# Last stage of a two-layer inference step: kept weight pieces, layer norm on VectorE, sample rows with the second projection

## Chip, cores and metric

The kernel runs on one core of one Trainium2 chip. The metric is the device time of one execution in microseconds, as the median of the runs.

## What is computed

One inference step of a two-layer model for a prompt of 1024 tokens and a group of 8 sample tokens, with the same weights. Only the second layer's end matters here: the recurrent mixer (RWKV-7) gives an output `y` for each token, gated by `silu(z)`, then comes one output projection by `w_out` (1024 x 1024), a residual and a layer norm.

```
def step(S, inp):                       # recurrence over the tokens, 16 heads of 64 x 64
    r_t, w_t, k_t, v_t, kk_t, a_t = inp
    sa = einsum('bhvk,bhk->bhv', S, kk_t)
    S = S * w_t[:, :, None, :] - sa[..., None] * (kk_t * a_t)[:, :, None, :] + v_t[..., None] * k_t[:, :, None, :]
    return S, einsum('bhvk,bhk->bhv', S, r_t)
...
out = (y.reshape(B, T, D_C) * silu(z)) @ w_out
...
xp = _layer_norm(ALPHA * xp + yp, ln_g[l], ln_b[l])    # prompt, 1024 rows
xq = _layer_norm(ALPHA * xq + ys, ln_g[l], ln_b[l])    # samples, 8 rows

def _layer_norm(x, g, b, eps=1e-5):
    mu = x.mean(-1); var = square(x - mu).mean(-1)
    return (x - mu) * rsqrt(var + eps) * g + b
```

## The kernel before

The kernel has four phases; the change lies in the last, `phase_d`, the second layer. It has two streams of work.

**The recurrence** runs in 16 units: 128 tokens (`g` = 0 to 7) by half of the heads (`d` = 0, 1). Each unit goes through generators: `s1` and `s2` prepare its matrices (`AM`, `BK`, `MRB`, `SV`, `KBK` and others, tiles of the unit pool `us` with three buffers, or of `up` with one), `joinUT` inverts a triangle, and `s3` carries the state `ST` through the unit in two chunks of 64 tokens. A chunk ends with the VectorE multiplication at L1547 (into `SV` after the first chunk, into `ST` after the second); a unit ends with its normed output `sq` (L1562, L1563), which goes to DRAM as `YT`, or, for the last unit, stays as `G.Y`.

**The projections** are generators in a list `F1`, from which the loop over the units takes about one step for each step of a unit: the gate projection for 512 tokens (`t_proj(.., "z", ..)`, into `SZ`) and `t_out(0)`, then again one and `t_out(1)`; `t_out(2)` joins the list at unit 13, `t_last` at unit 15. `t_out(g)` projects 256 tokens. It loads the recurrence's output (`og`) and the gate (`xs`) in 8 blocks of 128 features, multiplies and splits them in a high and a low part (`xh`, `xl`), and then goes over two halves `f` of the output and four pieces `k2` of the weights. For each piece, `wsplit` (L1172) loads 512 KB of `w_out` into a tile `w`, ScalarE makes the high part `wh` (L113) and GpSimd, or each third time VectorE, the low part `wl` (L121); three products of 512 columns follow for each row tile and k step (L1772 to L1774): `xh wh`, `xh wl`, `xl wh`. The pool of the weights has two buffers of each name. VectorE joins the sum with the residual (L1777) into the tile `big` and sums the rows; `ln_out` does the layer norm, with gain and bias rows loaded into tiles `w` of the same pool. In `t_out(2)` the 8 sample rows come along as a third row tile: 264 columns in place of 256, products into `sm`, residual and result in `xk`.

`t_last` does the last 256 tokens. They end only with the last unit, so it works on two tiles of 128 tokens: for the first tile, `tis` is (0,) throughout; the second goes with it for the pieces with `k2` under 2 and comes last for the other four, for which the four pieces are loaded and split again once `G.Y` is there (L1728). Its gain and bias rows lie in tiles `KBK` and `AM`.

The layer norm of a row tile before: mean; ScalarE's Square with a sum (L1655, its unneeded result in a tile `og`); variance; ScalarE's Ln and Exp (L1659, L1660), each with a table load ahead; three small VectorE operations; then over 1024 columns a VectorE pass for subtraction and scale (L1665), and two passes for gain (L1666) and bias (L1667), on GpSimd but for the last tile of `t_last`. Row tiles come one after the other.

The order of instructions on each engine is not written by hand: a scheduler goes over the generators' instructions with a model of their times and fixes one order for each engine, and each engine takes its queue in order. SP issues almost all loads and stores.

## Time and profile before

| | us |
|---|---|
| three runs | 2203.44, 2210.73, 2210.95 |
| median | 2210.73 |
| profiled execution | 2201.91 |
| its span | 2200.2 |

TensorE is busy for 1844.0 us of the span, VectorE for 1491.9, ScalarE for 1153.6 and GpSimd for 972.8. The mean granted clock of TensorE is 0.871 of full speed. The stage that the change touches begins at about 1826 us, when `t_out(0)` comes to its layer norm. The second projection's last join is at 1993, the third's at 2087, the recurrence's last output comes at 2162, and the program ends at 2200. In the rows further below, `PE` is TensorE, `DVE` VectorE, `ACT` ScalarE, `POOL` GpSimd, and `SPq` the queue of SyncE, which issues DMAs; a name left of an arrow is the tile written, those right of it are read.

### The profile page before, as it was taken

To read this page: it belongs to the slowest core of one execution; us is meant where nothing else is said; L and a number is where in the kernel's file an instruction comes from. 1 tells how busy PE (TensorE), PEld (TensorE's weight loads), DVE (VectorE), ACT (ScalarE), POOL (GpSimd) and SP (SyncE) were. 2 spreads that over 40 slices of the span, in tenths; PEclk is the share of its full clock that TensorE was granted. 3 is DMA by queue.
4 is the path that set the end of the run, shared out by engine and by line. 5 is a ranking of instruction groups with operands and counts; after the bars stand their busy time and mean duration, and the time that the engine had idled before them with its cause. 6 is when DMAs were issued, how large, how long until landed. Compare 5 with 4: busy or idle time off the path is not lost. (4 is left out here: it accounts for less than half of the span.)

```text
span 2200.2 us, 41365 instructions
## 1 busy us (share of the span) xinstructions
PE 1844.0 (84%) x16026; PEld 1545.8 (70%) x16026; DVE 1491.9 (68%) x2543; ACT 1153.6 (52%) x2359; POOL 972.8 (44%) x784
## 2 busy tenths in 40 slices
PE   5988897668999997897887999897999787987865
PEld 5987896656767886674777987695888666875543
DVE  5998995557788878226364378827748987387453
ACT  3323324544665545357466467747754575465344
POOL 4667667554655545445345212323334434113233
PEclk9998998867999876898898999897899986988956
DMA  6424344521221213546556344433544544353333
GB/s 240 132 72 142 131 151 154 200 74 33 65 59 50 58 34 97 175 126 210 167 179 204 126 118 116 145 100 117 149 130 121 180 115 135 97 155 115 119 112 103
DMA packets 232095, 275.27 MB, mean 125 GB/s; under 512 B 71545, under 2 KB 171569, under 8 KB 227738
## 3 DMA queue, kind: packets, MB, share of 16 engines
q1 hardware_dynamic: 210712, 215.21, 32.1%
q0 software_dynamic: 7616, 41.52, 5.6%
q10 hardware_dynamic: 13570, 15.90, 2.0%
q8 instruction: 126, 2.06, 0.4%
q14 instruction: 71, 0.58, 0.1%
HBM read 212.47 MB, written 64.27 MB: 126 GB/s over the span
## 5 line engine op out<-in xcount | busy, mean ns | idle before, releaser
L121 POOL TENSOR_TENSOR wl<-w,wh 128x1024 fp32r<-128x1024 f32 x81 | 200.2, 2473 | 333.5 <-ACT wh L113 317.8
L1184 PE MATMUL mm<-xh,wh 128*128 128x256 f32 (+1 forms) x1024 | 308.3, 302 | 22.6 <-ACT og L1319 9.3
L1185 PE MATMUL mm<-xl,wh 128*128 128x256 f32 (+1 forms) x1024 | 300.9, 294 | 2.0 <-POOL xl L1212 1.1
L1186 PE MATMUL mm<-xh,wl 128*128 128x256 f32 (+1 forms) x1024 | 298.5, 293 | 3.5 <-POOL wl L121 3.5
L113 ACT ACTIVATE wh<-w 128x1024 fp32r<-128x1024 f32 (+2 forms) x130 | 134.4, 1036 | 208.2 <-PE mm L1185 60.9
L1184 PEld LDWEIGHTS mm<-xh,wh 128*128 128x128 f32 x1024 | 201.9, 198 | 35.8 <-ACT og L1319 12.0
L1185 PEld LDWEIGHTS mm<-xl,wh 128*128 128x128 f32 x1024 | 203.2, 198 | 5.4 <-issue 2.0
L1186 PEld LDWEIGHTS mm<-xh,wl 128*128 128x128 f32 x1024 | 202.1, 198 | 6.3 <-POOL wl L121 4.4
L268 DVE SCALAR_TENSOR_TENSOR c<-U,cw,c 128x1024 f32<-128x1024 f32 x120 | 198.0, 1674 | 0.9
L604 POOL TENSOR_TENSOR Pl<-PT,Ph 128x512 fp32r<-128x512 f32 (+1 forms) x102 | 131.9, 1298 | 150.4 <-DVE Ph L603 123.9
L252 POOL TENSOR_TENSOR cbuf<-cbuf 128x256 f32<-128x256 f32 (+2 forms) x72 | 131.3, 1829 | 85.2 <-ACT cbuf L250 82.3
L217 PE MATMUL S<-xh,wh 128*128 128x344 f32 (+1 forms) x432 | 146.6, 339 | 21.1 <-ACT wh L113 19.4
L219 PE MATMUL S<-xh,wl 128*128 128x344 f32 (+1 forms) x432 | 145.4, 337 | 15.7 <-POOL wl L121 11.6
L218 PE MATMUL S<-xl,wh 128*128 128x344 f32 (+1 forms) x432 | 146.3, 339 | 3.8 <-POOL xl L121 3.6
L1212 POOL TENSOR_TENSOR xl<-xs,xh 128x520 fp32r<-128x520 f32 (+1 forms) x76 | 104.6, 1382 | 91.2 <-ACT xh L1211 89.1
L250 ACT ACTIVATE cbuf<-cbuf,wrow 128x256 f32<-128x256 f32 x192 | 79.3, 496 | 112.1 <-DMA cbuf<-in_ccmp,cix 70.3
L1208 DVE SCALAR_TENSOR_TENSOR xs<-xk,mu,xs 128x512 f32<-128x512 f32 x96 | 92.7, 973 | 56.4 <-ACT xs L1207 55.7
L217 PEld LDWEIGHTS S<-xh,wh 128*128 128x128 f32 (+1 forms) x432 | 85.6, 198 | 23.2 <-ACT wh L113 21.9
L562 DVE TENSOR_REDUCE nm<-S 128x1 f32<-128x640 f32 (+7 forms) x128 | 88.3, 699 | 18.9 <-PE S L558 17.7
L219 PEld LDWEIGHTS S<-xh,wl 128*128 128x128 f32 (+1 forms) x432 | 84.9, 197 | 20.1 <-POOL wl L121 13.6
L121 DVE TENSOR_TENSOR wl<-w,wh 128x1024 fp32r<-128x1024 f32 x45 | 60.4, 1341 | 54.1 <-ACT wh L113 53.9
L218 PEld LDWEIGHTS S<-xl,wh 128*128 128x128 f32 (+1 forms) x432 | 84.8, 196 | 7.1 <-POOL xl L121 4.4
(610 smaller groups left out, 5399.3 us busy)
## 6 DMA issues: line engine op xcount, KB each, us to landing
w<-in_w_rkvz SPq DMA_DIRECT2D x64, 512.0 KB
w<-in_w_out SPq DMA_DIRECT2D x36, 512.0 KB
w<-in_w_fm SPq DMA_DIRECT2D x25, 512.0 KB
xk<-x1T SPq DMA_DIRECT2D x48, 260.0 KB
xk<-x1T SPq DMA_DIRECT2D x48, 256.0 KB
w<-in_w_out SPq DMA_DIRECT2D x16, 256.0 KB
x<-in_xp SPq DMA_DIRECT2D x8, 512.0 KB
x<-x ACTq DMA_DIRECT2D x8, 512.0 KB
```

The costliest lines, as they stand in the source:

```text
L113: nc.scalar.activation(hi, src, AF.Copy, **({} if scale is None else {"scale": scale}))
L121: e_lo.tensor_tensor(lo, src, hi, op=SUB)
L217: nc.tensor.matmul(dst, lhsT=wh[:, k, 0:n], rhs=xh[:, k, sl], start=k == 0, stop=False)
L218: nc.tensor.matmul(dst, lhsT=wh[:, k, 0:n], rhs=xl[:, k, sl], start=False, stop=False)
L219: nc.tensor.matmul(dst, lhsT=wl[:, k, 0:n], rhs=xh[:, k, sl], start=False, stop=k == 7)
L252: nc.gpsimd.tensor_tensor(bv[:, 0:n], bv[:, 0:n], bv[:, n:2 * n], op=ADD)
L268: e.scalar_tensor_tensor(c[:, i, 0:T], u[:, k:k + T], cwh[:, i, k:k + 1], c[:, i, 0:T], op0=MUL, op1=ADD)
L604: lambda: nc.gpsimd.tensor_tensor(Pl[:, 0:w], PT[:, 0:w], Ph[:, 0:w], op=SUB)]
L1184: nc.tensor.matmul(dst, lhsT=wh[:, k], rhs=xh[k][:, lo:hi], start=k == 0, stop=False)
L1185: nc.tensor.matmul(dst, lhsT=wh[:, k], rhs=xl[k][:, lo:hi], start=False, stop=False)
L1186: nc.tensor.matmul(dst, lhsT=wl[:, k], rhs=xh[k][:, lo:hi], start=False, stop=k == 7)
L1212: (nc.vector if early[0] and k % LD == 0 else nc.gpsimd).tensor_tensor(lo[k][:, 0:n], t[:, 0:n], hi[k][:, 0:n], op=SUB)
```

## The change

Four things are changed, all in `phase_d`:

1. `wsplit` can write into tiles that are handed to it. `t_last` takes eight tiles of the unit pool (two each of `MRB`, `BK`, `SV` and `AM`) and keeps in them the split parts of the four pieces with `k2` of 2 and 3, so that the second tile uses these again: 8 loads and splits in place of 12. Its gain and bias rows move to tiles `w`.
2. `ln_out` goes over all row tiles stage by stage: all Squares, all Ln, all Exp. Two VectorE passes take the place of the three: (x - mean) times gain, then times the scale plus bias. The first is written ahead of the small operations on the scale, and GpSimd does nothing here any more.
3. The sample rows go with `t_out(1)` in place of `t_out(2)`.
4. At the start of `t_out(1)` the sample rows' own recurrence (`sample_d`) is run to its end, if it isn't there yet. Its last operation is at L1643.

```diff
--- before.py
+++ after.py
@@ -1169,11 +1169,10 @@
         def otile():
             return (OP[0] if early[0] else sp).tile([128, 520], F32, name="og")
 
-        def wsplit(src):
+        def wsplit(src, dst=None):
             w = wtile()
             nc.sync.dma_start(w, src)
-            wh = wp.tile([128, 8, 128], F32R, name="wh")
-            wl = wp.tile([128, 8, 128], F32R, name="wl")
+            wh, wl = dst or (wp.tile([128, 8, 128], F32R, name="wh"), wp.tile([128, 8, 128], F32R, name="wl"))
             cnt[0] += 1
             split(nc, wh, wl, w, nc.scalar, nc.vector if cnt[0] % (WD if early[0] else 3) == 0 else nc.gpsimd)
             return wh, wl
@@ -1643,28 +1642,31 @@
             nc.vector.tensor_tensor(G.ysn, w3(sq), bvs, op=ADD)
             yield
 
-        def ln_out(rows, parts_, st, gb, g, eng):
-            for ti, (o, r) in enumerate(rows):
-                parts = parts_[ti]
-                if parts is None:
-                    continue
-                s = lambda i: st[0:r, ti, i:i + 1]
+        def ln_out(rows, parts_, st, gb, g):
+            live = [ti for ti in range(len(rows)) if parts_[ti]]
+            S = lambda ti, i: st[0:rows[ti][1], ti, i:i + 1]
+            for ti in live:
+                r = rows[ti][1]
                 junk = sp.tile([128, D], BF, name="og")
-                nc.vector.tensor_scalar(s(2), s(0), s(1), -1.0 / D, op0=ADD, op1=MUL)
-                for i, (x, fs) in enumerate(parts):
-                    nc.scalar.activation(junk[0:r, fs], x[0:r], AF.Square, bias=s(2), accum_out=s(3 + i))
-                if len(parts) > 1:
-                    nc.vector.tensor_tensor(s(3), s(3), s(4), op=ADD)
-                nc.vector.tensor_scalar(s(4), s(3), 1.0 / D, LN_EPS, op0=MUL, op1=ADD)
-                nc.scalar.activation(s(5), s(4), AF.Ln)
-                nc.scalar.activation(s(5), s(5), AF.Exp, scale=-0.5)
-                nc.vector.tensor_tensor(s(6), s(5), s(5), op=MUL)
-                nc.vector.tensor_scalar(s(6), s(6), s(4), -0.5, op0=MUL, op1=MUL)
-                nc.vector.tensor_scalar(s(6), s(6), 1.5, s(5), op0=ADD, op1=MUL)
-                for x, fs in parts:
-                    nc.vector.tensor_scalar(x[0:r], x[0:r], s(2), s(6), op0=ADD, op1=MUL)
-                    eng[ti].tensor_tensor(x[0:r], x[0:r], gb[0][0:r, fs], op=MUL)
-                    eng[ti].tensor_tensor(x[0:r], x[0:r], gb[1][0:r, fs], op=ADD)
+                nc.vector.tensor_scalar(S(ti, 2), S(ti, 0), S(ti, 1), -1.0 / D, op0=ADD, op1=MUL)
+                for i, (x, fs) in enumerate(parts_[ti]):
+                    nc.scalar.activation(junk[0:r, fs], x[0:r], AF.Square, bias=S(ti, 2), accum_out=S(ti, 3 + i))
+                if len(parts_[ti]) > 1:
+                    nc.vector.tensor_tensor(S(ti, 3), S(ti, 3), S(ti, 4), op=ADD)
+                nc.vector.tensor_scalar(S(ti, 4), S(ti, 3), 1.0 / D, LN_EPS, op0=MUL, op1=ADD)
+            for ti in live:
+                nc.scalar.activation(S(ti, 5), S(ti, 4), AF.Ln)
+            for ti in live:
+                nc.scalar.activation(S(ti, 5), S(ti, 5), AF.Exp, scale=-0.5)
+            for ti in live:
+                o, r = rows[ti]
+                for x, fs in parts_[ti]:
+                    nc.vector.scalar_tensor_tensor(x[0:r], x[0:r], S(ti, 2), gb[0][0:r, fs], op0=ADD, op1=MUL)
+                nc.vector.tensor_tensor(S(ti, 6), S(ti, 5), S(ti, 5), op=MUL)
+                nc.vector.tensor_scalar(S(ti, 6), S(ti, 6), S(ti, 4), -0.5, op0=MUL, op1=MUL)
+                nc.vector.tensor_scalar(S(ti, 6), S(ti, 6), 1.5, S(ti, 5), op0=ADD, op1=MUL)
+                for x, fs in parts_[ti]:
+                    nc.vector.scalar_tensor_tensor(x[0:r], x[0:r], S(ti, 6), gb[1][0:r, fs], op0=MUL, op1=ADD)
                     nc.sync.dma_start(O["y_s"][:, fs] if ti == 2 else O["y_p"][g * 256 + o:g * 256 + o + 128], x[0:r])
 
         def t_last():
@@ -1691,8 +1693,14 @@
             st = sp.tile([128, 3, 8], F32, name="st")
             p = [[q.tile([128, 512], F32, name=nm) for q, nm in r] for r in (((ps, "mm"), (ps, "mm")), ((pm, "sm"), (pa_, "pa")))]
 
+            kept = {}
+            slots = [us.tile([128, 1536 if nm == "AM" else 1024], F32R, name=nm, bufs=B[5])[:, 0:D]
+                     .rearrange("p (a b) -> p a b", b=128) for nm in ("MRB", "BK", "SV", "AM") for _ in range(2)]
+
             def part(f, k2, tis):
-                wh, wl = wsplit(I["w_out1"][f, k2])
+                if k2 >= 2 and (f, k2) not in kept:
+                    kept[f, k2] = wsplit(I["w_out1"][f, k2], (slots.pop(), slots.pop()))
+                wh, wl = kept[f, k2] if k2 >= 2 else wsplit(I["w_out1"][f, k2])
                 for k in range(2):
                     a, b = (w[:, 4 * k:4 * k + 4].rearrange("p a b -> p (a b)") for w in (wh, wl))
                     kk = 2 * k2 + k
@@ -1712,13 +1720,11 @@
                 for f in range(2):
                     part(f, k2, (0, 1) if k2 < 2 else (0,))
                 yield
-            gb = []
-            for i in (1, 3):
-                gb.append((up if i == 1 else us).tile([128, 1536], F32, name="KBK" if i == 1 else "AM",
-                                                      bufs=B[0] if i == 1 else B[5])[:, 0:D])
-                nc.sync.dma_start(gb[-1], I["ln_rows"][i:i + 1].to_broadcast([128, D]))
+            gb = [flat(wtile()) for _ in range(2)]
+            for t, i in zip(gb, (1, 3)):
+                nc.sync.dma_start(t, I["ln_rows"][i:i + 1].to_broadcast([128, D]))
             join(0)
-            ln_out([(0, 128)], [[(h[0], slice(0, D))]], st, gb, 3, [nc.gpsimd])
+            ln_out([(0, 128)], [[(h[0], slice(0, D))]], st, gb, 3)
             yield
             while not hasattr(G, "Y"):
                 yield
@@ -1728,33 +1734,35 @@
                 for f in range(2):
                     part(f, k2, (1,))
             join(1)
-            ln_out([(0, 128), (128, 128)], [None, [(h[1], slice(0, D))]], st, gb, 3, [None, nc.vector])
+            ln_out([(0, 128), (128, 128)], [None, [(h[1], slice(0, D))]], st, gb, 3)
             yield
 
         def t_out(g):
-            n = 264 if g == 2 else 256
+            n = 264 if g == 1 else 256
             y = xpair()
+            if g == 1:
+                run(F3, 1000)
             for j in range(8):
                 y[0].append(xp.tile([128, 264], F32R, name="xh"))
                 y[1].append(xp.tile([128, 264], F32R, name="xl"))
                 og = sp.tile([128, 264], F32, name="og")
                 nc.sync.dma_start(og[:, 0:256], YT[g][j // 4][:, j % 4])
-                if g == 2:
+                if g == 1:
                     nc.gpsimd.tensor_copy(og[:, 256:264], G.ysn[:, j])
                 sz = sp.tile([128, 264], F32, name="xs")
                 nc.sync.dma_start(sz[:, 0:256], SZ[g][:, j, 0:256])
-                if g == 2:
+                if g == 1:
                     nc.sync.dma_start(sz[:, 256:264], SZ[3][:, j, 256:264])
                 nc.vector.scalar_tensor_tensor(sz[:, 0:n], og[:, 0:n], V(j, 4), sz[:, 0:n], op0=ADD, op1=MUL)
                 split(nc, y[0][j][:, 0:n], y[1][j][:, 0:n], sz[:, 0:n], nc.scalar, nc.vector, scale=0.5)
                 if j % 2:
                     yield
-            rows = [(0, 128), (128, 128)] + ([(256, NS)] if g == 2 else [])
+            rows = [(0, 128), (128, 128)] + ([(256, NS)] if g == 1 else [])
             h = [bp.tile([128, D], F32, name="big") for _ in range(2)]
             for ti in range(2):
                 nc.sync.dma_start(h[ti], scr["x1"][2 * g + ti])
             H = [[x[:, 0:512], x[:, 512:]] for x in h]
-            if g == 2:
+            if g == 1:
                 H.append([one.tile([128, 512], F32, name="xk", bufs=3) for _ in range(2)])
                 for f in range(2):
                     nc.sync.dma_start(H[2][f][0:NS], scr["x1"][8][0:NS, f * 512:f * 512 + 512])
@@ -1782,7 +1790,7 @@
                 nc.sync.dma_start(gb[-1], I["ln_rows"][i:i + 1].to_broadcast([128, D]))
             parts = [[(h[ti], slice(0, D))] if ti < 2 else [(H[2][f], slice(f * 512, f * 512 + 512)) for f in range(2)]
                      for ti in range(len(rows))]
-            ln_out(rows, parts, st, gb, g, [nc.vector if g == 3 and ti else nc.gpsimd for ti in range(len(rows))])
+            ln_out(rows, parts, st, gb, g)
             yield
 
         def run(gens, cost):
```

What this does to the order is shown at three places. The first is VectorE's queue from the third projection's last join on (`big` and `mm` at L1777; L1547 is the end of a recurrence chunk, L1665 the layer norm's pass). Before:

```order
L1777 SCALAR_TENSOR_TENSOR big,st<-big,mm 128x512 x2
L1653 TENSOR_SCALAR st<-st 128x1
L1777 SCALAR_TENSOR_TENSOR xk,st<-xk,sm 8x512
L1653 TENSOR_SCALAR st<-st 128x1
L1653 TENSOR_SCALAR st<-st 8x1
L1547 TENSOR_TENSOR SV<-pB,PC 64x4x64 x2
L1658 TENSOR_SCALAR st<-st 128x1 x2
```

After, from the last small operations of that layer norm on (L1669 is its second pass, L1546 the end of a chunk):

```order
L1666 TENSOR_SCALAR st<-st 128x1
L119 SCALAR_TENSOR_TENSOR xl<-xs,xh 128x128
L1666 TENSOR_SCALAR st<-st 128x1
L1667 TENSOR_SCALAR st<-st 128x1
L119 SCALAR_TENSOR_TENSOR xl<-xs,xh 128x128
L1667 TENSOR_SCALAR st<-st 128x1
L1489 COPY UT<-pg 16x8x16
L1669 SCALAR_TENSOR_TENSOR big<-big,st,w 128x1024 x2
L1489 COPY UT<-pg 16x8x16
L1493 STREAM_TRANSPOSE U<-UT 128x256
L1682 SCALAR_TENSOR_TENSOR xs<-og,vec,xs 128x128 x2
L1546 TENSOR_TENSOR SV<-pB,PC 64x4x64 x2
```

The end of this chunk of unit 14 stood right behind the join and now stands behind the second passes of both tiles.

The second place is ScalarE's queue in the same layer norm, after the change (L1653 is Square, L1658 Ln, L1660 Exp):

```order
L1653 ACTIVATE og,st<-big,st 128x1024 x2
L1658 ACT_TABLE_LOAD
L1658 ACTIVATE st<-st 128x1
L1660 ACT_TABLE_LOAD
L1660 ACTIVATE st<-st 128x1
L1537 ACTIVATE SV<-pA 64x4x64
L1658 ACT_TABLE_LOAD
L1658 ACTIVATE st<-st 128x1
L1660 ACT_TABLE_LOAD
L1660 ACTIVATE st<-st 128x1
```

The two tiles' Square stand together, their Ln and Exp still alternate.

The third is the end of SP's queue (`w<-in_w_out` is a piece of the weights, `xs<-sz` a gate block, `out_wkv_p` the last state of the recurrence). Before:

```order
L1174 DMA w<-in_w_out 128x1024 x2
L1679 DMA og<-yt_9137 128x128 x2
L1676 DMA xs<-sz_9130 128x128 x4
L1174 DMA w<-in_w_out 128x1024 x3
L1848 DMA out_wkv_p<-ST 128x512
L1174 DMA w<-in_w_out 128x1024 x3
L1676 DMA xs<-sz_9130 128x128 x2
L1174 DMA w<-in_w_out 128x1024 x2
L1668 DMA out_y_p<-big 128x1024 x2
```

After:

```order
L1681 DMA og<-yt_9137 128x128 x4
L1678 DMA xs<-sz_9130 128x128 x4
L1174 DMA w<-in_w_out 128x1024 x3
L1856 DMA out_wkv_p<-ST 128x512
L1174 DMA w<-in_w_out 128x1024
L1725 DMA w<-in_ln_rows 128x1024 x2
L1678 DMA xs<-sz_9130 128x128 x2
L1670 DMA out_y_p<-big 128x1024 x2
```

Five of the loads of `w_out` stood behind the store of the state, one does now, with the loads of gain and bias behind it.

## Rows read from the trace of the kernel before

**Rows 1.** Part 1 of the page: TensorE's busy time, share of the span, and count of instructions.

```profile
PE 1844.0 (84%) x16026; PEld 1545.8 (70%) x16026; DVE 1491.9 (68%) x2543; ACT 1153.6 (52%) x2359; POOL 972.8 (44%) x784
```

**Rows 2.** The table of stretches from 1960 us on: the stretch and its length, busy time and instruction count of TensorE, its weight loads, VectorE, ScalarE and GpSimd, the granted clock, the share of the DMA engines and GB/s.

```profile
1960.00:1980.00 20.00, 16.11 (x125) 13.15 (x125) 17.81 (x34) 11.54 (x20) 3.50 (x3) 0.83 0.53 154
1980.00:2000.00 20.00, 18.43 (x353) 13.21 (x354) 9.27 (x22) 10.67 (x23) 6.65 (x8) 1.00 0.22 74
2000.00:2020.00 20.00, 11.30 (x104) 8.24 (x104) 16.51 (x26) 15.43 (x32) 10.76 (x7) 0.70 0.20 49
2020.00:2040.00 20.00, 13.05 (x111) 9.55 (x112) 16.23 (x35) 5.86 (x10) 5.51 (x6) 0.76 0.74 246
2040.00:2060.00 20.00, 20.00 (x257) 12.84 (x255) 9.29 (x19) 5.80 (x13) 5.61 (x5) 0.86 0.46 143
2060.00:2080.00 20.00, 20.00 (x190) 13.26 (x182) 12.31 (x26) 10.92 (x22) 4.29 (x2) 1.00 0.34 100
2100.00:2120.00 20.00, 6.19 (x67) 3.72 (x66) 18.08 (x24) 3.62 (x13) 15.21 (x8) 0.50 0.13 33
```

**Rows 3.** The chain of waits that ended last, in order of time: start in us, length in us, what it was. Between 2029 and 2200 us, the pieces that the text speaks of.

```profile
2029.31 6.40 DMA w<-in_w_out
...
2048.07 0.23 PE sm L1772
...
2084.77 1.71 DMA UT<-ud
...
2087.15 1.30 DVE big L1777 x4
...
2101.80 2.78 DVE big L1665
...
2122.27 3.74 DMA w<-in_w_out
...
2166.98 2.62 DMA xs<-sz
...
2176.83 3.30 POOL big L1666
...
2182.57 2.31 POOLq L1962
```

**Rows 4.** The layer norm's passes over the tile `big`, by line and engine, from 1800 us on: count, then shortest, median and longest in ns, first and last start in us, shapes.

```profile
L1665 DVE TENSOR_SCALAR big<-big,st x8: 803/815/2862, 1829.2 to 2193.1; 128x1024 f32<-128x1024 f32 x8
L1666 POOL TENSOR_TENSOR big<-big,w x6: 2342/2467/2862, 1830.1 to 2104.7; 128x1024 f32<-128x1024 f32 x6
L1667 POOL TENSOR_TENSOR big<-big,w x6: 2333/2378/2881, 1837.6 to 2113.0; 128x1024 f32<-128x1024 f32 x6
```

**Rows 5.** VectorE's timeline from 1830 us on: start in us, length in us (of all of them where it says x2), line, operation, tiles and shapes; in brackets the idle time before it and what ended it.

```profile
1830.11 2.58 DVE L1433 TENSOR_TENSOR XT<-XI,MT 64x64 f32<-64x64 f32 x2
...
1838.28 5.00 DVE L1373 TENSOR_TENSOR AM<-kk,P 64x512 f32<-64x512 f32 x2
...
1992.78 0.69 DVE L1777 SCALAR_TENSOR_TENSOR big<-big,mm 128x512 f32<-128x512 f32 x1
...
2008.11 2.86 DVE L1665 TENSOR_SCALAR big<-big,st 128x1024 f32<-128x1024 f32 x1
...
2011.95 2.38 DVE L1369 SCALAR_TENSOR_TENSOR at<-at,kk 128x512 f32<-128x512 f32 x1
2014.25 3.53 DVE L1373 TENSOR_TENSOR AM<-kk,P 64x512 f32<-64x512 f32 x2
...
2019.70 2.72 DVE L1562 TENSOR_TENSOR sq<-Y,sq 128x512 f32<-128x512 f32 x1
...
2089.35 0.86 DVE L1547 TENSOR_TENSOR SV<-pB,PC 64x256 f32<-64x256 f32 x2
...
2109.95 3.20 DVE L119 SCALAR_TENSOR_TENSOR xl<-xs,xh 128x128 fp32r<-128x128 f32 x1
...
2152.22 0.85 DVE L1547 TENSOR_TENSOR ST<-pB,PC 64x256 f32<-64x256 f32 x2 [1.49 <-PE pB L1521]
...
2161.39 0.69 DVE L1563 TENSOR_TENSOR sq<-sq,bv 128x512 f32<-128x512 f32 x1
...
2162.72 3.29 DVE L121 TENSOR_TENSOR wl<-w,wh 128x1024 fp32r<-128x1024 f32 x1
...
2195.17 1.23 DVE L1667 TENSOR_TENSOR big<-big,AM 128x1024 f32<-128x1024 f32 x1
```

**Rows 6.** SP's timeline: issue of loads of `w_out`, start and length in us.

```profile
2018.75 0.38 SPq L1174 DMA_DIRECT2D w<-in_w_out  x1
...
2155.31 11.06 SPq L1174 DMA_DIRECT2D w<-in_w_out  x3
...
2167.87 6.69 SPq L1174 DMA_DIRECT2D w<-in_w_out  x2
```

**Rows 7.** The timelines of TensorE (the last two products) and of ScalarE (the last tile's Square and the table load for Ln).

```profile
2185.99 0.63 PE L1702 MATMUL pa<-wl,xh 128*128 128x512 f32 x1
2186.42 0.63 PE L1703 MATMUL pa<-wh,xl 128*128 128x512 f32 x1
...
2188.07 1.15 ACT L1655 ACTIVATE og<-big,st 128x1024 bf16<-128x1024 f32 x1 [7.79 <-DVE st L1653]
...
2189.32 1.28 ACT L1659 ACT_TABLE_LOAD   x1
```

## The prediction

> **What bounds the kernel now.** I read the page's shares first [rows 1]: TensorE is busy in 84% of the span, so it is the nearest bound as a mean; the change, though, touches only the last 380 us, so I went to the table of stretches [rows 2]. There TensorE is full between 2040 and 2080 (20.00 of 20 us) and idle by a third to two thirds elsewhere: 8.70 us idle in 2000 to 2020, 6.95 in 2020 to 2040, 13.81 in 2100 to 2120. Two things run there side by side: the recurrence (units of 128 tokens and half the heads, one after another) and, put between its steps, the output projections of 256 tokens each, with a layer norm behind each. The chain of waits [rows 3] says what ends last. It goes through a load of w_out at 2029.31 (6.40 us), the transposed values of the recurrence's last unit at 2084.77 and the join of the third projection at 2087.15, a VectorE pass of its layer norm at 2101.80 (2.78), another load of w_out at 2122.27, and from 2166.98 on through the last projection alone: gate rows by DMA, then a GpSimd pass of the layer norm at 2176.83, and at 2182.57 the queue behind it. So this stretch hangs on chains between engines, not on any engine's sum of work.
>
> **The layer norm.** Before, each tile of 128 tokens takes a VectorE pass (0.81 us) and two on GpSimd (2.47 and 2.38) [rows 4]. After, it takes two VectorE passes of two inputs, which the trace has only as the last tile's own: 1.23 each [rows 5]. So VectorE gets 2 x 1.23 - 0.81 = 1.65 us more a tile, 3.3 for two. What it gets back shows in its timeline [rows 5]: operations that lie beside a GpSimd pass are stretched. A two-input operation of 512 elements takes 0.69 alone; beside GpSimd 2.38, 2.72 and (two of them) 5.00 and 3.53. The pass of 0.81 takes 2.86.
> - First layer norm, at 1830 to 1843: 5.00 - 1.38 = 3.6, and about 2 from the pair of 64x64 operations (2.58), which I estimate at 0.5 when free, since they have an eighth of the 0.69's elements and a start of their own. Net 5.6 - 3.3 = -2.3. I take **-2** (-4 to 0; TensorE waits here for the chain of the recurrence, so not all need come through).
> - Second layer norm, at 2008 to 2022: 2.86, 2.38, 3.53 (two) and 2.72 are 2.05 + 1.69 + 2.15 + 2.03 = 7.9 too long, against +3.3; the sample rows' layer norm, which now lies here too, adds two halves of two passes of 0.69 and some ten small operations, some 5 us. VectorE: about nothing.
>
> One row of the same timeline speaks against it: a two-input split of 1024 elements on VectorE at 2162.72 took 3.29 us [rows 5] while GpSimd did the other split of a weight; the layer norm's last tile, with no split beside it, took 1.23. The Trainium skill ("SBUF — State Buffer", Who interferes with whom) states why the new passes keep this risk: VectorE shares a pair of ports with GpSimd, and an instruction with two SBUF inputs contends with any GpSimd instruction that reads SBUF. By that rule, with 12 passes in three layer norms and GpSimd at weight splits for about a quarter of the time, it would be 3 meetings of 3.29 - 1.23 = 2.1 us, and the sum below would be -21 instead of -27. My sum takes 1.23 all the same, since how often they meet is not seen before they run.
>
> **The sample rows.** Eight rows more cost 48 matmuls (8 k steps, two halves of the output, three products), since a matmul's time goes by its 512 columns: 0.23 us each at the higher clock [rows 3], 11.0 us of TensorE, with VectorE's two joins, 8 small GpSimd copies and 12 DMAs on SP (8 gate rows, 2 residuals, 2 outputs; at 0.38 a piece [rows 6] 4.6 us of its queue, beside TensorE's work). All leave the third projection and enter the second. There TensorE stands idle for 3.89 + 1.57 = 5.5 us between 1960 and 2000 [rows 2], so **+8** until the second projection's join (5.5 to 11).
>
> **From that join (1993.4) to the third one (2087.15).** The 48 matmuls are gone where TensorE was full: -11. The 15.7 us of idle TensorE in 2000 to 2040 are a wait for the third projection's weights. Their first load, at 2018.75 [rows 6], has to wait for a tile of the weights' pool that holds the layer norm's gain, free only after GpSimd's first pass; after the change the gain is read for the last time by VectorE's first pass, which needs neither Ln nor Exp: join 1.3, Square 2 x 1.15 [rows 7], pass 1.23, so about 2000, 18 us earlier. SP's own queue ahead of it (gate rows whose tiles come free as TensorE goes on) will hold some of that: half of the idle, -8. Together **-19**; the ends are -8 (the matmuls' time goes into waiting for the recurrence, whose transposes are due at the same 2087) and -27 (all of the idle).
>
> **From the third join to the recurrence's last output (2162.1), 75 us.** Gone are the stretched 2.78 and 3.20 [rows 3, 5], 2.0 and (one of 128 elements, at most 0.3 when free) 2.9, and the sample rows' layer norm (on VectorE some 3 us); added are 3.3. The next load, at 2122.27, stood on SP behind GpSimd's last pass, with TensorE idle 13.81 of 20 us; now it waits for VectorE's first pass. Against that the order shows the join further ahead of the recurrence: the piece of it that ended at 2089.35, 2 us behind the join, now ends behind the whole third layer norm. From that end to the last one, at 2152.22, three pieces took 63 us, 21 each [rows 5], and nothing in the change shortens a piece as such. So what the join gains ahead of the recurrence comes back here, up to 10 us of it. I take **0** (-10 to +10).
>
> **The tail, from 2162.1 to the end (38.1 us).** Before, three loads of w_out are issued at 2155.31 and two at 2167.87, the four weights of the second tile are split again, GpSimd's split of the last waits behind its two layer-norm passes (2182.57 in the chain), and TensorE does its last products at 2185.99 and 2186.42 [rows 3, 6, 7]. After, the four weights lie split in tiles of the units' pool, so only the gate rows for the last four blocks are missing. Step by step: join of the first tile 0.7; gate rows 2.62 by DMA behind 1.3 of the pair before; a wait behind the first tile's Square, Ln and Exp on ScalarE, about 2.9; twelve products, 0.43 apart, = 5.1; join 0.7; Square 1.15 and two table loads of 1.28 with their operations, 4.4; small operations 0.9; one pass 1.23 (the other lies beside Ln and Exp); and the output's DMA, which took the 3.8 us from the last pass to the end. Together 23.7: **-14** (-17 to -10). The cover of the kept weights is that they were split while the recurrence still ran; if they come later than 2162, each costs a split of 2.4 on GpSimd.
>
> **Sum.** -2 + 8 - 19 + 0 - 14 = -27 us on the profiled 2201.9: 2175. The three runs lie 1.5 to 9 us above the profiled execution; with half of the 9 a median of 2179. Of what the change says, one piece hardly happens: in the order, the third layer norm still has Ln, Exp, another operation, Ln, Exp on ScalarE, four table loads. With two it would be 2.6 us less; that is counted at nothing.
>
> **The rivals.**
> - Tail only. The recurrence, and not the projections, sets 2087 and 2162. For it: the chain goes through the last unit's transposes just ahead of the join. Then +8 is made up again by the -11, all else is nought, and -14 remains: 2188 profiled, 2192 as a median.
> - Larger. Both middle stretches come out at their far ends (-27, -10): -2 + 8 - 27 - 10 - 14 = -45, 2157, or 2161 as a median. For it speaks the idle TensorE in 2000 to 2040 and 2100 to 2120.
> - No gain: 2200 to 2215 as a median. The tail's 14 us are given back in the middle, where the sample rows' 11 delay the second join and the third projection is then paced by its loads as before.
> - Slower. VectorE takes its queue in order, and the piece of unit 14 that before ended 2 us behind the third join now stands behind that layer norm, whose passes wait for Square, Ln and Exp. That piece is then late by the 10 us of the upper end above; and the tiles of the units' pool that the kept weights take come free only as unit 14 ends. If for this their loads are issued later than about 2150 in the old trace's terms, four splits of 2.4 on GpSimd, 9.9 us, run behind the recurrence, with the first tile's join and layer norm behind them, and the tail is as long as before. The sample rows' 11 us come back nowhere: -2 + 11 + 0 + 10 + 0 = +19, 2221, or 2225 as a median. Against it: before, five loads were issued after 2155, and by the order one or two at most are left to come behind the recurrence's last state.
>
> **How the numbers follow.** My forecast gets 0.40 (2165 to 2190 by its own terms), tail only 0.25, larger 0.15, no gain 0.12, slower 0.08. The range reaches from the larger case to the near half of no gain, 2155 to 2206, and leaves out some 2 in 10: the slower case, the far half of no gain and a little on the low side. 0.5% (11 us, so from 2200 to 2222) is what a measurement here can tell from no change. Faster: larger, nearly all of the forecast and four fifths of tail only, 0.73; same: the rest of these and no gain, 0.19; slower 0.08.
>
> **What would show it.** In the changed trace, no layer-norm pass on GpSimd and no VectorE operation of 2 us or more in the three layer norms; the second projection's last join 4 to 8 us later; the third one's first load within 10 us of that join, and TensorE's idle in the 40 us behind it halved; no load of w_out after the recurrence's last output, and some 24 us from there to the end; no wait of TensorE for a split there. I am wrong in the middle if the stretch between the joins is as long as before though its 48 matmuls are gone, and in the tail if the kept splits end after the recurrence.

## The result and the profile after

The changed kernel takes 2174.16 us as a median (2172.18 to 2177.47, 4 runs), the kernel before 2210.84 (2203.44 to 2213.54, 4 runs beside it). The ratio is 0.9848, with a 95% interval of 0.982 to 0.9875: 28 to 40 us faster. The forecast was 2179 in a range of 2155 to 2206, with most of the chance on faster. The profiled execution took 2172.46 us with a span of 2170.4.

To see where the time went, I cut the last part of each profile at four events on VectorE: the first join of the first projection (M), the last join of the second (J1) and of the third (J2), and the last addition of the last unit of the recurrence (T). Up to M the instructions are the same in both kernels, and the two executions are nevertheless 5.2 us apart there. VectorE's timeline before has M and J2:

```profile
1784.18 0.69 DVE L1777 SCALAR_TENSOR_TENSOR big<-big,mm 128x512 f32<-128x512 f32 x1
...
2087.77 0.68 DVE L1777 SCALAR_TENSOR_TENSOR big<-big,mm 128x512 f32<-128x512 f32 x1
```

VectorE's timeline after has M, J1, J2 and T:

```profile
1789.40 0.69 DVE L1785 SCALAR_TENSOR_TENSOR big<-big,mm 128x512 f32<-128x512 f32 x1
...
2005.80 0.69 DVE L1785 SCALAR_TENSOR_TENSOR big<-big,mm 128x512 f32<-128x512 f32 x1
...
2076.98 0.69 DVE L1785 SCALAR_TENSOR_TENSOR big<-big,mm 128x512 f32<-128x512 f32 x1
...
2148.16 0.69 DVE L1562 TENSOR_TENSOR sq<-sq,bv 128x512 f32<-128x512 f32 x1
```

So each stretch is compared from its own M. Before, J1 starts at 1992.78 and T at 2161.39 [rows 5]. From M to the end the change is worth 35.0 us; the two spans show 29.8, since the later M takes 5.2 of it back. That the spans lie near the forecast of -27 is in part chance.

| us | M to J1 | J1 to J2 | J2 to T | T to end | M to end |
|---|---|---|---|---|---|
| before | 208.6 | 95.0 | 73.6 | 38.8 | 416.0 |
| changed | 216.4 | 71.2 | 71.2 | 22.2 | 381.0 |
| difference | +7.8 | -23.8 | -2.4 | -16.6 | -35.0 |
| forecast | +6 | -19 | 0 | -14 | -27 |

The layer norm's passes in the view of the tile `big` after (shortest, median, longest in ns): all on VectorE, and one of the 16 stretched (L1664 is the first pass, which reads the gain, L1669 the second, which reads the bias).

```profile
L1664 DVE SCALAR_TENSOR_TENSOR big<-big,st,w x8: 1266/1276/1286, 1824.4 to 2161.5; 128x1024 f32<-128x1024 f32 x8
L1669 DVE SCALAR_TENSOR_TENSOR big<-big,st,w x8: 1269/1280/3130, 1838.1 to 2165.1; 128x1024 f32<-128x1024 f32 x8
```

That one is the row at 1840.56 of VectorE's timeline, and beside it GpSimd's has a split of a weight:

```profile
1840.56 3.13 DVE L1669 SCALAR_TENSOR_TENSOR big<-big,st,w 128x1024 f32<-128x1024 f32 x1
```

```profile
1840.26 2.35 POOL L121 TENSOR_TENSOR wl<-w,wh 128x1024 fp32r<-128x1024 f32 x1
```

So one sign of the prediction, no VectorE operation of 2 us or more in the three layer norms, failed here, and once more at 2031.93, where an operation into `KBK` took 2.87 beside another split.

SP's timeline after: the third projection's first weights, the last projection's first, and the kept pieces with the gain and bias rows behind them.

```profile
2013.21 0.33 SPq L1174 DMA_DIRECT2D w<-in_w_out  x1
...
2086.52 0.33 SPq L1174 DMA_DIRECT2D w<-in_w_out  x1
...
2129.51 7.40 SPq L1174 DMA_DIRECT2D w<-in_w_out  x3
...
2139.03 0.33 SPq L1174 DMA_DIRECT2D w<-in_w_out  x1
2143.46 3.69 SPq L1725 DMA_DIRECT2D w<-in_ln_rows  x2
```

The first comes 7 us behind J1 (before 26), the second 9.5 behind J2 (before 34.5), and none behind T. What they waited for shows in the last passes that read the gain, whose tile `w` the load takes over. VectorE's timeline after has them:

```profile
2012.45 0.73 DVE L1664 SCALAR_TENSOR_TENSOR xk<-xk,st,w 8x512 f32<-8x512 f32 x1
...
2085.22 1.27 DVE L1664 SCALAR_TENSOR_TENSOR big<-big,st,w 128x1024 f32<-128x1024 f32 x1
```

GpSimd's timeline before:

```profile
2011.06 2.72 POOL L1666 TENSOR_TENSOR big<-big,w 128x1024 f32<-128x1024 f32 x1
...
2111.74 1.25 POOL L1666 TENSOR_TENSOR xk<-xk,w 8x512 f32<-8x512 f32 x1
```

After, both loads are issued 0.03 us behind the end of that pass. Before, they are issued at 2018.75 [rows 6] and 2122.27 [rows 3], 5.0 and 9.3 us behind it: for that time the tile was free, and the loads stood behind other transfers in SP's queue, the second one behind gate blocks that waited for VectorE's splits `xl`.

TensorE's idle time in the 40 us that begin 7 us behind J1 is 4.2 us where it was 15.7 [rows 2]:

```profile
2013.00:2033.00 20.00, 17.13 (x130) 13.16 (x129) 14.77 (x34) 15.85 (x34) 2.25 (x2) 0.58 0.47 132
2033.00:2053.00 20.00, 18.64 (x210) 13.93 (x208) 19.67 (x41) 8.54 (x19) 6.47 (x3) 0.99 0.76 250
```

### The profile page after: what moved, and what is told of

Read it like the earlier page. It is cut to its first block, busy times and chain, and to the rows that moved or that the text cites. A ratio compares the mean times of both kernels' runs of the same rounds, so it can differ in the third digit from the quotient of the medians.

```text
span 2170.4 us, 41322 instructions
## 1 busy us (share of the span) xinstructions
PE 1842.0 (85%) x16026; PEld 1541.4 (71%) x16026; DVE 1487.7 (69%) x2550; ACT 1149.7 (53%) x2355; POOL 932.7 (43%) x763
## 5 line engine op out<-in xcount | busy, mean ns | idle before, releaser
L121 POOL TENSOR_TENSOR wl<-w,wh 128x1024 fp32r<-128x1024 f32 x76 | 189.6, 2496 | 329.6 <-ACT wh L113 313.9
L113 ACT ACTIVATE wh<-w 128x1024 fp32r<-128x1024 f32 (+1 forms) x122 | 126.1, 1035 | 176.4 <-DMA w<-in_w_fm 61.8
L217 PE MATMUL S<-xh,wh 128*128 128x344 f32 (+1 forms) x432 | 147.4, 341 | 22.6 <-ACT wh L113 20.2
L217 PEld LDWEIGHTS S<-xh,wh 128*128 128x128 f32 (+1 forms) x432 | 85.4, 198 | 24.9 <-ACT wh L113 23.4
L562 DVE TENSOR_REDUCE nm<-S 128x1 f32<-128x640 f32 (+7 forms) x128 | 88.3, 699 | 16.6 <-PE S L558 15.6
L602 ACT ACTIVATE PT<-mm 128x512 f32<-128x512 f32 (+1 forms) x102 | 59.4, 586 | 60.0 <-PE mm L590 42.5
```

The source lines that it names most:

```text
L113: nc.scalar.activation(hi, src, AF.Copy, **({} if scale is None else {"scale": scale}))
L121: e_lo.tensor_tensor(lo, src, hi, op=SUB)
L217: nc.tensor.matmul(dst, lhsT=wh[:, k, 0:n], rhs=xh[:, k, sl], start=k == 0, stop=False)
```

## The experiments

The two theories behind most of them: the parts pay separately and add (A), or they need each other (B); and, for the layer norm, the cost before was GpSimd's work beside VectorE (C), or the weights' tiles that were held by it, so that late weights stood in TensorE's queue (R). All times in the table at the end of this section are profiles cut as above; each is one execution of its kernel, and up to J1, where several kernels are alike, they repeat to 1.7 us. The ratios of the times give the same differences against the kernel before as M to end does, to 4.5 us, so a smaller difference between two kernels is not shown by them.

**One part alone.** The kept pieces (`wsplit` with `dst`, `t_last` with `kept`, `slots` and gain and bias in `wtile()`):

```diff
+                if k2 >= 2 and (f, k2) not in kept:
+                    kept[f, k2] = wsplit(I["w_out1"][f, k2], (slots.pop(), slots.pop()))
+                wh, wl = kept[f, k2] if k2 >= 2 else wsplit(I["w_out1"][f, k2])
```

> The kept weight pieces alone (with gain and bias of the last layer norm in tiles of the weights' pool), layer norm and sample rows as before. Theory A, the parts pay separately, each in its own stretch: the tail from the recurrence's last output to the end shrinks from 38 to 24 us and nothing else moves: -14 (-17 to -10). Theory B, the parts need each other: with the layer norm's passes still on GpSimd the kept splits queue behind the third layer norm's passes and end after the recurrence: -6 or less, and a tail above 30 us.

The ratio is 0.9943 (0.9908 to 0.9978). The tail is 23.5 us, 15.3 less, and the rest is as before to 1.8 us: theory A, with the size of the forecast.

The layer norm alone (`ln_out` as changed, nothing else):

> The layer norm in two VectorE passes alone. Theory A: -4 at the first layer norm, -8 to -12 between the second and third join (weights of the third projection load earlier), -3 in the tail, where no GpSimd pass holds up the last split: -15 to -20. Theory B: VectorE's longer queue gives back what contention cost, and TensorE is full in the third projection with its sample rows: the third join moves by less than 4 us, -4 to -8 in all.

0.991 (0.9877 to 0.9942). In all -20.4, as A had it, but not where: -3.6 until J1, -0.8 from J1 to J2, -14.5 from J2 to T, -1.5 in the tail.

The sample rows alone:

```diff
-            n = 264 if g == 2 else 256
+            n = 264 if g == 1 else 256
```

(and likewise at the other `g == 2`, with `run(F3, 1000)` ahead).

> The sample rows with the second projection alone. Theory A: +11 until the second join, -11 between it and the third, no change behind: 0 (-4 to +4). Theory B: their leaving the full third projection and the third layer norm is what shortened the middle: +8, -15, -4, so -10 or more.

1.0004 (0.9974 to 1.0033): no difference. +12.1 until J1, given back as -2.2 and -11.6, and 3.5 more in the tail. Here GpSimd's last passes over the gain in the second layer norm are those of the sample rows; they end 41 us behind J1, and the third projection's first load comes 44.8 behind it.

**One part undone.** The changed kernel with the sample rows back in the third projection:

> The changed kernel with the sample rows back in the third projection. Theory A: the second join 11 us earlier, the third one as in the changed kernel: within 4 us of the changed kernel (-40 to -32 against before). Theory B: the middle loses most of its gain: about 10 us slower than the changed kernel (-26 against before).

0.9842 (0.9795 to 0.9889), the same as the changed kernel; M to end 380.3 against 381.0. Its middle differs: 91.1 and 59.7 where the changed kernel has 71.2 and 71.2. Theory A.

With the old layer norm (kept pieces, and sample rows with the second projection):

> The changed kernel with the old layer norm on GpSimd. If the parts add, it is the kernel before less the 12 to 16 us of the kept pieces: the stretch to the recurrence's last output 375 to 378, the tail 24 to 28, -10 to -14 in all. If the kept splits come late behind GpSimd's passes (the rival in which the tail is as long as before): tail 34 or more, no gain.

0.9966 (0.9943 to 0.999), and here the parts do not add: the tail is 37.1 us though the pieces are kept. The timelines of SP and then of GpSimd in this kernel show why; T is at 2160.42:

```profile
2151.38 5.96 SPq L1174 DMA_DIRECT2D w<-in_w_out  x3
...
2165.06 0.37 SPq L1174 DMA_DIRECT2D w<-in_w_out  x1
```

```profile
2160.69 2.62 POOL L121 TENSOR_TENSOR SV<-w,SV 128x1024 fp32r<-128x1024 f32 x1 [6.99 <-ACT SV L113]
...
2165.09 2.38 POOL L121 TENSOR_TENSOR BK<-w,BK 128x1024 fp32r<-128x1024 f32 x1 [1.78 <-ACT BK L113]
```

The kept pieces' loads are issued from 9 us ahead of T to 5 behind it, so splits run behind T. In the changed kernel the same loads are issued 18.7 and 9.1 us ahead, in the kernel with the kept pieces alone 17.0 and 7.6, by SP's timeline there (T at 2170.54):

```profile
2153.53 5.97 SPq L1174 DMA_DIRECT2D w<-in_w_out  x3
...
2162.98 0.33 SPq L1174 DMA_DIRECT2D w<-in_w_out  x1
```

The kernel with the kept pieces alone has the old layer norm too, and there they come in time. Counted from J2, the old layer norm with moved rows has its loads no later (49.5 to 63.1 us behind J2, with the kept pieces alone 56.6 to 66.1); it is T that comes sooner, 58.5 us behind J2 in place of 73.6.

Without the kept pieces:

> The changed kernel without the kept pieces. If the kept pieces pay in the tail alone: to the recurrence's last output as in the changed kernel (359 from the first projection's first join, 356 to 362), tail 35 to 39 in place of 22, -18 to -22 against before in all. If the layer norm's early weights paid only together with them: that stretch 365 or more, and -12 or less in all.

0.9933 (0.9908 to 0.9958), -18.1 in the profile; to T 363.7, a little above what was expected, and a tail of 34.2, a little below. So the kept pieces are worth 16.9 us in the changed kernel, 12.0 of it in the tail and 4.9 ahead of T.

**What in the layer norm pays.** All three are the layer norm alone, altered. Their ratios, in the order of the text, are 0.9918 (0.989 to 0.9946), 0.9891 (0.9858 to 0.9923) and 0.994 (0.9914 to 0.9967); none differs from the 0.991 of the layer norm alone by more than the intervals allow, so what follows rests on the stretches of the profiles. With GpSimd passes that nobody waits for and that hold no tile of the weights' pool:

```diff
+                    if g < 3:
+                        for _ in range(4 * (fs.stop - fs.start) // D):
+                            nc.gpsimd.tensor_tensor(gh[0:r], cc[0:r, 0:512], S(ti, 6).to_broadcast([r, 512]), op=MUL)
```

> The two VectorE passes alone, and beside them four GpSimd passes of 512 columns a tile (constants times the scale, into a tile that nobody reads) in the first three layer norms: as much GpSimd time as before beside VectorE and ahead of the weights' splits, but no tile of the weights' pool is held. Same stretch. Theory C: 370 to 378. Theory R: 358 to 365.

M to T 362.6: theory R. All of the difference from the layer norm alone is ahead of J1, +5.8 us; from J1 to the end this kernel takes 190.3, the layer norm alone 190.6, the kernel before 207.4. VectorE's and GpSimd's timelines of this kernel in the first layer norm show one place where it costs:

```profile
1846.63 2.38 DVE L1433 TENSOR_TENSOR XT<-XI,MT 64x64 f32<-64x64 f32 x2
```

```profile
1845.59 2.02 POOL L1675 TENSOR_TENSOR gh<-cc,st 128x512 f32<-128x512 f32 x1
```

VectorE's timeline of the layer norm alone has the same pair without such a pass beside it:

```profile
1838.26 1.52 DVE L1433 TENSOR_TENSOR XT<-XI,MT 64x64 f32<-64x64 f32 x2
```

The pair of 64x64 operations beside a pass into `gh` takes 2.38 in place of 1.52; beside the old pass it took 2.58 [rows 5]. Operation by operation against the layer norm alone, VectorE's operations beside these passes are longer by 3.7, 5.3 and 3.1 us in the three layer norms. In the second that is two thirds of the 7.9 us that the prediction counted before, so the old stretching is put back in part, and what is put back behind J1, 8.4 us, costs nothing there. The passes also keep splits waiting in GpSimd's queue; how the 5.8 us ahead of J1 divide between the two is not known.

With the first pass made to wait for the scale:

```diff
+                nc.vector.scalar_tensor_tensor(S(ti, 7), S(ti, 6), 0.0, S(ti, 2), op0=MUL, op1=ADD)
+                for x, fs in parts_[ti]:
+                    nc.vector.scalar_tensor_tensor(x[0:r], x[0:r], S(ti, 7), gb[0][0:r, fs], op0=ADD, op1=MUL)
```

> The two VectorE passes alone, with the first pass made to wait for the scale (it takes the mean from a copy that is made behind Ln, Exp and the small operations). GpSimd stays free of the layer norm, but the gain's tile, and with it the next weights' load, comes free some 10 us later. Time from the first projection's first join to the recurrence's last output: before 377, two passes alone 358. Theory C (contention with GpSimd was the cost): 357 to 361. Theory R (late weights hold up TensorE's queue, and the recurrence's products stand in it): 366 to 374.

M to T is 366.1, 7.8 more than with the passes alone and just inside R's range; but the tail is 30.3 in place of 37.3, and M to end 396.4 against 395.6. The first loads come 22.6 us behind J1 and 21.9 behind J2, where with the passes alone it is 16.7 and 7.5, and the end comes no later. The reading that fits is that without kept pieces the last projection's twelve loads end the kernel, not the recurrence; no run tests it.

With the three old passes on VectorE (L1665 to L1667 of the code before, on `nc.vector`):

> The layer norm with the old three passes, all of them on VectorE, the rows still staged: 3.3 us of VectorE a tile in place of 2.5, GpSimd free of it, the gain's tile free only behind Ln, Exp and the second pass. Same stretch. Theory C: 359 to 363. Theory R: 367 to 375, a little more than with the late first pass.

M to T 365.1, between the two ranges: undecided. 5.1 us more until J1, 3.5 more behind it. Two things here speak against a simple account. GpSimd is free of the layer norm, and yet M to J1 is 210.1, no less than before (208.6). And the third projection's first load comes 33.1 us behind J1, 7 later than before, and yet J1 to end is 194.1, 13.3 less than before.

**The late first pass in one layer norm of the kernel with all parts.**

```diff
+                if g == 2:
+                    nc.vector.scalar_tensor_tensor(m, S(ti, 6), 0.0, S(ti, 2), op0=MUL, op1=ADD)
+                    for x, fs in parts_[ti]:
+                        nc.vector.scalar_tensor_tensor(x[0:r], x[0:r], m, gb[0][0:r, fs], op0=ADD, op1=MUL)
```

(the pass ahead of the small operations falls away there).

> The changed kernel, but in the third layer norm alone the first pass waits for the scale. In the changed kernel the last projection's first weights are asked for 9.5 us after the third join, and 93 us pass from that join to the end. Theory R (that load sets when the kept pieces are split and how long TensorE's queue stands): load some 20 us after the join, the stretch from the third join to the end +6 to +9, nothing changed ahead of it. Theory C (only the GpSimd passes beside VectorE counted): within 2 us of the changed kernel.

0.9838 (0.9794 to 0.9883); J2 to end 94.4 against 93.4. The last projection's first load is 10 us later behind J2, and nothing follows: R is wrong for the third layer norm, once the kernel keeps its pieces, for a delay of this size.

The same for `g == 1`:

> The changed kernel, but in the second layer norm alone the first pass waits for the scale. With the two passes alone a late first pass shortened the stretch between the second and third join by 5.8 us, against theory R. If that came from the second layer norm itself: -6 between these joins here too, and a faster kernel by up to 6 us. If it came from how the scheduler's order happened to fall: between -2 and +8, by theory R, since the third projection's first weights are asked for later.

0.9896 (0.9856 to 0.9935), M to end +10.1: 17.0 more from J1 to J2, 7.4 less behind. VectorE's timeline has the join and the first pass, SP's the third projection's first load:

```profile
2007.89 0.69 DVE L1792 SCALAR_TENSOR_TENSOR big<-big,mm 128x512 f32<-128x512 f32 x1
...
2033.49 1.27 DVE L1674 SCALAR_TENSOR_TENSOR big<-big,st,w 128x1024 f32<-128x1024 f32 x1
```

```profile
2045.09 0.38 SPq L1174 DMA_DIRECT2D w<-in_w_out  x1
```

The first pass comes 26 us behind the join, where in the changed kernel it came 2 us behind it, and the third projection's first load 37 us behind, where it came 7. This is more than the wait for the scale: the scheduler also put the sample rows' passes, the last ones that read the gain, far back, and the load is issued 0.1 us behind them. R holds here, by a little more than the 8 us expected at most. By the ratios the difference is 10.6 us, and the two intervals just overlap.

> The same late first pass of the second layer norm in the kernel with the sample rows left in the third projection. Same two readings: -6 between the second and third join and up to 6 us faster than that kernel (2166), or -2 to +8.

0.9867 (0.9831 to 0.9904), +6.2 against the kernel without the moved rows; -1.0 from J1 to J2, +10.5 to T, -3.7 in the tail. This is R's range again; by the ratios it is 5.5 us, and their intervals overlap widely, so the profile alone carries it. No version was found that beats the changed kernel by more than the measurement tells.

| us | M to J1 | J1 to J2 | J2 to T | T to end | M to end |
|---|---|---|---|---|---|
| kept pieces alone | 208.6 | 96.7 | 73.6 | 23.5 | 402.4 |
| layer norm alone | 205.0 | 94.2 | 59.1 | 37.3 | 395.6 |
| sample rows alone | 220.7 | 92.8 | 62.0 | 42.3 | 417.9 |
| without sample rows' move | 204.5 | 91.1 | 59.7 | 25.0 | 380.3 |
| without new layer norm | 221.0 | 95.0 | 58.5 | 37.1 | 411.6 |
| without kept pieces | 215.2 | 71.6 | 76.8 | 34.2 | 397.9 |
| layer norm, GpSimd passes beside | 210.8 | 95.1 | 56.7 | 38.4 | 401.1 |
| layer norm, first pass late | 204.4 | 88.4 | 73.4 | 30.3 | 396.4 |
| layer norm, three passes | 210.1 | 91.1 | 63.9 | 39.1 | 404.2 |
| all, third norm's pass late | 216.3 | 70.4 | 69.5 | 24.9 | 381.1 |
| all, second norm's pass late | 216.9 | 88.2 | 61.0 | 25.1 | 391.1 |
| without the move, second norm's late | 204.9 | 90.1 | 70.2 | 21.3 | 386.5 |

## Why the prediction was right, and where its steps were not

- **First layer norm, -2.** Right and a little small: M to J1 is 3.6 to 5.5 us less in the four pairs of kernels that differ in the layer norm alone. That GpSimd's passes cost time there is shown: with them put back beside, +5.8. That freeing GpSimd is enough is not: with three passes on VectorE the gain is gone too (210.1), so VectorE's own queue counts as well.
- **The sample rows, +8 and -11.** Moving them cost 10.2 to 12.4 us until the second join in four pairs of kernels, all of the 11.0 or nearly, and little or none of it hidden in the 5.5 us of idle TensorE that I subtracted; this comes back behind J1: 164.6 us from there to the end with the move, 175.8 without it. The net is 0.7, 1.9 and 2.3 us of loss in three pairs, less than can be told from nothing, and 9.2 in the fourth, where the kept pieces then come too late: the move is worth nothing, where the sum had -3.
- **Earlier weights, -8, between second and third join.** The mechanism is shown in the kernel with all parts: with the second norm's first pass late, +10.1 (and, less surely, +6.2 without the moved rows). With the rows moved, J1 to J2 also follows the first load over six kernels: load 7 us behind J1, 70.4 to 71.6; 37 behind, 88.2; 44 to 45 behind, 92.8 and 95.0. With the rows unmoved it does not: loads 16 to 33 us behind J1 and 88.4 to 96.7 without order. The place was wrong. With the rows where they were, the third join hardly moves (95.0 to 94.2, kept pieces 96.7 to 91.1), and the gain shows behind it; with the rows moved it shows ahead of it. The third join was not a point that the end hung on, so my cut at it split one gain into two terms that each came out wrong: -19 and 0 where -23.8 and -2.4 were measured.
- **From the third join on, 0.** The -2.4 is near it, but by luck, for the step behind it failed: "nothing in the change shortens a piece as such". The piece that I feared for did end later, 20.6 us behind J2 in place of 1.6, 19 us later where I allowed 10. But from its end to the last one the three pieces took 39.0 us, where before they took 62.9 [rows 5]. VectorE's timeline after has both ends:

```profile
2097.58 0.88 DVE L1546 TENSOR_TENSOR SV<-pB,PC 64x256 f32<-64x256 f32 x2
...
2136.59 0.86 DVE L1546 TENSOR_TENSOR ST<-pB,PC 64x256 f32<-64x256 f32 x2
```

  Of the 26.2 us that the change gains from J1 to T, 23.9 lie in these three pieces. The layer norm alone shortens them to 45.1, the sample rows alone to 48.5, the kept pieces alone hardly (61.5). Why they are shorter is open in the main. I put 4.9 us of stretched operations there on the side of the gain; the run with GpSimd's passes beside put 3.1 back there and 5.3 ahead of J2, and lost nothing by it (190.3 from J1 to the end, 190.6 without). That speaks against GpSimd's time beside VectorE as what pays the 16.8 us of the layer norm alone behind J1, though not all of that time was put back. The other reading is the tiles of the weights, and with them the time of the loads. It is shown for the second layer norm of the changed kernel; two runs speak against it as the whole cause: a late first pass in all norms of the kernel without kept pieces changed its end by 0.8 us, and with three passes on VectorE most of the gain stayed although the third projection's first load came later than before. How the rest divides between the gain's and the bias's tile, and the order that the scheduler gives, stays open. Nor was it GpSimd's last pass that the load at 2122.27 stood behind on SP, as I wrote: the gain's tile was free 9.3 us earlier.
- **The tail, -14.** -16.6; -15.3 by the kept pieces alone. The sum of 23.7 was near the 22.2, but two of its steps were wrong, and that they cancel is luck: I put 2.9 us for a wait behind the first tile's layer norm and 5.1 for twelve products; TensorE did not wait there, and 24 products ran behind T, since the four kept pieces meet the second tile only then. They took 8.6 us. The splits of the last blocks did stand behind Square, Ln and Exp on ScalarE, until 2155.3, but the first twelve products ran until then. Nor were three loads issued at 2155.31 before: that row covers 11.06 us, and one of them was issued at 2166.05. TensorE's timeline has the first and the last of the 24 products, their starts 8.2 us apart:

```profile
2150.12 0.80 PE L1709 MATMUL sm<-AM,xh 128*128 128x512 f32 x1 [1.85 <-ACT xh L113]
...
2158.35 0.40 PE L1711 MATMUL pa<-MRB,xl 128*128 128x512 f32 x1
```

- **The rival that the kept pieces come too late** is real: it is the kernel with the old layer norm and moved rows, with a tail of 37.1. It did not cost the +19 that I gave it, since the recurrence's end came no later. In the changed kernel the new layer norm keeps the loads far enough ahead, which is the one place where the parts are shown to need each other: the new layer norm is worth 20.0 to 22.1 us in the three kernels without that trouble, and 30.6 with it.
- **New passes beside splits, counted at nothing.** One of the 16 passes met a split and took 3.13 us in place of 1.28, where my other count had three of twelve. The rule of the Trainium skill ("SBUF — State Buffer", Who interferes with whom) that a VectorE instruction with two SBUF inputs contends with a GpSimd instruction that reads SBUF agrees with this row.

## What to carry to other kernels

A tile that a slow engine reads last holds up whoever loads into it next; before counting an engine's time, ask which pool its last read releases, how long behind the join that is, and what stands ahead of the waiting load in its own queue. A chain of equal pieces need not keep its length: here the same three pieces of the recurrence took 39 us in one kernel and 63 in another. A cut at an event that the end does not hang on gives terms that may each be wrong while their sum is right; take the sum between events that do. Keeping data instead of loading it again pays in the tail only if its load and split end ahead of the event that the tail starts from.

## What was not expected of the hardware

The time at which the last stage begins differs from execution to execution by more than most parts of the change are worth: in the profiles here M lies between 1780.3 and 1798.2 us though no instruction ahead of it is changed, while the same instructions from M to J1 then take 208.6 us in two different kernels. And TensorE ran the first half of the tail's products at the lower clock of 1.2 GHz, with the granted clock at 0.50, after 5 us in which it was busy for 1.93; the tail's sum had taken this spacing for its twelve products. The table of stretches of the changed kernel has it:

```profile
2145.00:2150.00 5.00, 1.93 (x6) 1.05 (x6) 4.32 (x10) 2.62 (x4) 0.00 (x0) 0.94 0.46 173
2150.00:2155.00 5.00, 4.88 (x12) 3.86 (x13) 2.76 (x9) 4.64 (x10) 0.00 (x0) 0.50 0.13 26
2155.00:2160.00 5.00, 3.74 (x14) 2.68 (x12) 3.25 (x10) 0.31 (x1) 0.00 (x0) 0.87 0.27 107
```

From the second product to 2156.26 they stood 0.43 us apart, from there on 0.23.
